# An encoder block on one Trainium2 core: two steps of the MLP's first product in plain float32 instead of split operands

## The chip, the cores and the metric

The kernel runs on one core of a Trainium2 chip, as one launch. A core has a matrix engine (TensorE, PE in the profile, with its weight loads PEld), a vector engine (DVE), a scalar engine (ACT), a general engine (GpSimd, POOL) and a queue engine (SyncE, SP), each with a program of its own that it runs in order, and 16 DMA engines between the main memory and the on-chip memory SBUF. Matrix products land in the banks of PSUM. The metric is the device time of one execution in microseconds (us), the median of several runs.

## The reference

One layer of a bidirectional encoder, 2048 rows of 1024 columns in float32. A mixing part (mLSTM heads and a long convolution) gives `mix`; then

```python
        mix = jnp.concatenate([y_m, y_h], axis=-1).astype(x.dtype) @ w_out
        x = x + rms_norm(mix, norm_mix_post)

        hm = rms_norm(x, norm_mlp_pre)
        ff = jnp.square(jax.nn.relu(hm @ w_mlp_in)) @ w_mlp_out
        x = x + rms_norm(ff, norm_mlp_post)
```

`w_mlp_in` is 1024 x 4096. The change is in the product `hm @ w_mlp_in`, the MLP's first.

## The kernel before

**Split products.** A float32 product is made of three matmuls of a faster type, fp32r. `split` writes each operand as hi + lo: hi is a cast (ACT, L166), lo the source less hi (DVE or POOL, L169). `mm3` then issues hi of one with lo of the other (L159), lo with hi (L160), hi with hi (L161). Given an operand that is not split, `mm3` issues one plain float32 matmul instead (L157); the profile shows a plain matmul as two records.

**Seven block products.** The first product is made in 32 steps. Step s takes the 256 columns number s % 16 of `w_mlp_in` and one half of the rows: the first half (1024 rows) in steps 0 to 15, the second in 16 to 31. A step is a 2 x 2 product by the Strassen-Winograd scheme: seven block products in the order 1, 2, 6, 5, 7, 4, 3, each of four blocks of 128 x 128 (weights) by 128 x 512 (rows). So a split step is 7 x 4 x 3 = 84 matmuls.

- The right operand of product i is one of seven combinations of the finished rows. `turn_out` (L1366 on) makes them for each pair of row blocks: PE turns the rows (L1373), DVE scales them (L1374), POOL combines them (L1389 to L1392), and they are stored to main memory in `ht`. `right_load` fetches combination i of a half into the tile that is to hold lo (named hm11 for i = 1, and so on), and `right_split` then puts hi into its other tile (hm10) and subtracts in place. Each split is made in two parts; the second goes to POOL where that is given. The seven operands of a half serve 16 steps.
- The weights of a step are made in `up_weights`: two loads (512 KB each), combinations on POOL (L1492, L1493, L1499, L1502), splits (ACT, POOL) into tiles of a pool named cb, which has nine places. A step's weights are split while the step before runs; its loads are issued a step earlier, after product 2 (`then`, in `up`).
- After each product DVE or ACT takes the result from its bank (L1669 for product 1 on ACT, L1656 for the others on DVE), the last sums are made at L1693 to L1695 and stored.

**The join with the output projection.** `out_proj` walks over 16 blocks of 128 rows. In each, POOL and DVE finish a group of `y` (L1267), PE turns it (L1273) and multiplies it with `w_out` (`part`: matmuls po), DVE and ACT evict with the norm (L1215 to L1221, in `post`), POOL adds the residual (L1222), ACT and DVE make the next norm (L1360 to L1363, in `normed`), and two rounds later the rows are turned out. PE, DVE and ACT follow the order in which this is written; POOL and SP follow the scheduler's. Step 0 of the first product is woven into the last rounds: `first_operands` loads hm1 and hm2, splits them, and loads, combines and splits the weights of step 0 after row blocks 11 to 14, in the scratch tiles wr and ws; `first_step` runs step 0 with tiles named m0 between the turns of row blocks 14 and 15, splitting hm6, hm5, hm7, hm4 and hm3 as they come. Steps from 1 on are `up`. At step 15, `then` loads the operands of the second half product by product, and splits them two products behind.

Of the kernel before, what the change touches and what calls it, by code (L numbers as in the profile page):

```python
# [8 lines left out]
F32 = mybir.dt.float32  # L9
F32R = mybir.dt.float32r  # L10
AF = mybir.ActivationFunctionType
ALU = mybir.AluOpType
# [135 lines left out]
class Builder:  # L148
# [1137 lines left out]
    def out_proj(self, c):  # L1286
# [129 lines left out]
        ys = {}  # L1416
        self.load(wb, io["norm_mix_post"].partition_broadcast(128))
        xns = {}
        staged = self.first_operands(scratch)
        wl = c.enter_context(tc.tile_pool(name="owl", bufs=2, side="right"))  # L1420
        for i in range(18):
            with tc.manual_schedule(engines={mybir.EngineType.PE,mybir.EngineType.DVE,mybir.EngineType.Activation}):
                if i == 0:
                    ys[1] = mixed(1)
                    zs[2] = gate(2)
                    part(pos[0], 0, ym[0], 0)
                    ym[1] = turned(ys.pop(1), 1, 1)
# [12 lines left out]
                if 0 < i < 16:  # L1440
                    xns[i - 1] = normed(i - 1, *done)
                    part(pos[i], 0, ym[i], 0)
                    if i + 2 < 16:
                        ys[i + 2] = mixed(i + 2)
                    if i > 1:
                        part(pos[i], 1, yz[i], 4)
                if 2 <= i:
                    turn_out(i - 2, xns.pop(i - 2))
                if i < 15:
                    part(pos[i], 1, ym[i], 0)  # L1450
                    done = finish(i, pos.pop(i))
                elif i == 15:

                    step = self.first_step(c, pp)
                    next(step)
                    part(pos[i], 1, ym[i], 0)
                    next(step)
                    rows = finish(i, pos.pop(i))
                    next(step)
                    xns[i] = normed(i, *rows)  # L1460
                else:
                    next(step)
            if 10 < i < 15:
                next(staged)
            if i == 14:
                gc.close()
            yield
        c.close()

# [13 lines left out]
    def up_weights(self, s, raw, s12, pieces=False):  # L1483
# [7 lines left out]
        cbs, cs = [], []  # L1491
        pool.tensor_tensor(s12[:, 0], a21, a22, ALU.add)  # L1492
        pool.tensor_tensor(a21, a11, a21, ALU.subtract)  # L1493
# [34 lines left out]
    def first_operands(self, scratch):  # L1528
# [9 lines left out]
        next(g)  # L1538
        yield
        self.w1_first = next(g)  # L1540
        yield

    def first_step(self, c, pp):

        wk = c.enter_context(self.tc.tile_pool(name="m0", bufs=1))
        count = [0]

        def tile(shape, tag):
            return wk.tile(list(shape), F32, tag=tag, name="m0", bufs={"g": 3, "s": 1, "r": 3}[tag])

        def bank():
            count[0] += 1
            if count[0] in (1, 2, 4, 5):
                return self.h1p.tile([128, 512], F32, tag="h1", name="pm")
            return pp.tile([128, 512], F32, tag="po", name="pm", bufs=3)

        for i in (6, 5):
            self.right_load(0, i)
        nxt = self.up_weights(1, [tile((128, 4, 256), "r") for _ in range(2)], tile((128, 2, 4, 128), "r"), True)
        next(nxt)  # L1560
        yield
        for i in (7, 4, 3):
            self.right_load(0, i)
        products = self.up_step(0, self.w1_first, lambda: tile((128, 2, 512), "g"), lambda: tile((128, 512), "s"), bank,
                                lambda i: None)
        next(products)
        next(products)
        self.right_split(6, self.pool)
        yield
        self.right_split(5, self.pool)  # L1570
        next(products)
        next(nxt)
        yield
        self.right_split(7)
        next(products)
        self.right_split(4)
        next(products)
        next(nxt)
        self.right_split(3)
        next(products)  # L1580
        yield
        for _ in products:
            pass
        self.w1 = next(nxt)
        yield

    def mlp(self):
        tc, io = self.tc, self.io
# [26 lines left out]
    def up(self, ring, next_bank, down):  # L1615
# [2 lines left out]

        def weights(s):
            raw = [ring((128, 4, 256), 1) for _ in range(2)]  # L1620
            g = self.up_weights(s % 16, raw, ring((128, 2, 4, 128), 1))
            next(g)
            return g

        def then(i):
            nonlocal nxt, w1
            if i == 2:
                if s + 1 < n:
                    w1 = next(nxt)
                if s + 2 < n:  # L1630
                    nxt = weights(s + 2)
            if s == 15:
                self.right_load(1, i)
                loaded.append(i)
            if len(loaded) > (2 if s == 15 else 0):
                j = loaded.pop(0)
                self.right_split(j, pool if j in (2, 7, 3) else None)
            if s == n - 1 and i in (2, 7):
                next(down)

        loaded = []
        w1, nxt = self.w1, weights(2)
        for s in range(1, n):
            for _ in self.up_step(s, w1, lambda: ring((128, 2, 512), 0),
                                  lambda: self.mk.tile([128, 512], F32, tag="mc", name="m4"), next_bank, then):
                pass

    def up_step(self, s, w, pair, single, next_bank, then):

        pe, dve, act, pool = self.pe, self.dve, self.act, self.pool  # L1650
        ga = self.ga[s % 16, s // 16]
# [11 lines left out]
        for i in (1, 2, 6, 5, 7, 4, 3):  # L1663
            pt = next_bank()
            hi, lo = self.hm[i]
            for k in range(4):
                self.mm3(pt, w(i, k), (hi[:, k, :], lo[:, k, :]), k == 0, k == 3)
            if i == 1:
                act.copy(c11, pt)  # L1669
            elif i == 2:  # L1670
# [248 lines left out]
```

## Time and profile before

| | us |
|---|---|
| median of 3 runs (2743.41 to 2745.59) | 2744.96 |
| the profiled run | 2740.85 |
| its span, from the first to the last instruction | 2738.9 |
| DVE busy in the span | 1529.3 |
| ACT busy | 1239.9 |
| POOL busy | 1218.2 |

The mean clock granted to PE is 0.981 of full speed. Rows of the timeline begin with the start and the length of a group of instructions; in square brackets stands how long the engine was idle before it, and what ended that. Matmuls overlap in the profile: the start of the next one says how long one takes. Rows of groups give the line, engine, operation, output and inputs with shapes, the count, the busy time, the mean in ns, and the idle time ahead of them.

### The profile page before, as it was taken

What the parts mean: (1) busy time and instruction counts of PE and PEld (TensorE: products, weight loads), DVE (VectorE), ACT (ScalarE), POOL (GpSimd) and SP (SyncE); (2) the same over time, 40 slices, a digit from 0 to 9 for tenths busy, and PEclk for the clock granted to TensorE, in tenths of its full rate; (3) what the DMA queues carried; (4) which work ended last, traced back from release to release, by engine and by line L of the source; (5) the groups of instructions that cost most, each with busy time, mean ns of one, the idle gap of its engine ahead of it and who ended that gap; (6) DMA issues with size and microseconds to landing.
All of it is one profiled execution on the core that took longest, in us unless ns stands there. A gap on an engine that the chain in (4) does not pass through costs nothing.

```text
span 2738.9 us, 35521 instructions
## 1 busy us (share of the span) xinstructions
PE 2604.2 (95%) x12293; PEld 2125.6 (78%) x12293; DVE 1529.3 (56%) x2453; ACT 1239.9 (45%) x2301; POOL 1218.2 (44%) x973
## 2 busy tenths in 40 slices
PE   6999999999899998889997999989999999999998
PEld 5778888777788887767775788868888888888876
DVE  5676653777446654765555444464445443543578
ACT  6355544555434445653433544354454233232244
POOL 1221124554225542456675877777773340311232
PEclk9999999999999999999998999989999999999999
DMA  6233346565665648546756444453446553445546
GB/s 173 59 97 107 113 122 226 183 191 175 203 216 180 191 156 273 166 145 209 239 165 220 149 168 143 167 210 139 162 144 253 176 182 110 123 143 164 181 160 222
DMA packets 288355, 465.76 MB, mean 170 GB/s; under 512 B 37542, under 2 KB 149414, under 8 KB 287152
## 3 DMA queue, kind: packets, MB, share of 16 engines
q1 hardware_dynamic: 227600, 324.85, 37.9%
q10 hardware_dynamic: 53264, 117.53, 11.4%
q0 software_dynamic: 7312, 21.11, 3.0%
q8 instruction: 98, 1.61, 0.2%
q14 instruction: 81, 0.66, 0.1%
HBM read 289.27 MB, written 174.13 MB: 169 GB/s over the span
## 4 chain that ended last, share of the span: by engine, by line
PE 40%; DVE 5%; POOL 3%; ACT 2%; DMA 2%; issue 2%; ACTq 0%; DVEq 0%; POOLq 0%; SPq 0%
PE pm L160 13%; PE pm L161 13%; PE pm L159 13%; DVE cb L169 1%; DVE hm L169 1%; POOL xt L1222 1%; ACT xo L1360 1%; DMA m<-in_w_mlp_out_dram 0%; DVE hm L1844 0%; POOL cb L169 0%; DVE xo L1363 0%; DMA hm<-ht 0%; ACTq L234 0%; DVE gss L1264 0%; POOL ht L1395 0%
## 5 line engine op out<-in xcount | busy, mean ns | idle before, releaser
L166 ACT CAST cb<-m 128x1024 fp32r<-128x1024 f32 (+1 forms) x346 | 281.3, 847 | 443.7 <-PE pm L159 388.6
L169 DVE TENSOR_TENSOR cb<-m,cb 128x1024 fp32r<-128x1024 f32 (+1 forms) x222 | 239.5, 1116 | 301.1 <-ACT cb L166 300.8
L160 PE MATMUL pm<-hm,cb 128*128 128x512 f32 x896 | 355.2, 396 | 18.8 <-DVE hm L169 14.7
L159 PE MATMUL pm<-hm,cb 128*128 128x512 f32 x896 | 354.5, 396 | 9.2 <-POOL cb L169 4.1
L161 PE MATMUL pm<-hm,cb 128*128 128x512 f32 x896 | 353.8, 395 | 0.0
L160 PE MATMUL pm<-cb 128*128 128x512 f32 x880 | 344.0, 391 | 6.5 <-DVE cb L169 6.5
L159 PE MATMUL pm<-cb 128*128 128x512 f32 x880 | 342.6, 390 | 1.0 <-DVE cb L169 1.0
L161 PE MATMUL pm<-cb 128*128 128x512 f32 x880 | 343.1, 390 | 0.0
L169 POOL TENSOR_TENSOR cb<-m,cb 128x1024 fp32r<-128x1024 f32 x124 | 268.7, 2180 | 71.0 <-ACT cb L166 71.0
L1656 DVE TENSOR_TENSOR m<-pm,m 128x512 f32<-128x512 f32 x224 | 154.4, 690 | 258.0 <-PE pm L161 231.3
L159 PE MATMUL pt<-hn,w 128*128 128x512 f32 x640 | 269.4, 421 | 1.0 <-ACT hn L486 0.9
L160 PE MATMUL pt<-hn,w 128*128 128x512 f32 x640 | 253.9, 397 | 0.7 <-DVE hn L487 0.7
L161 PE MATMUL pt<-hn,w 128*128 128x512 f32 x640 | 252.8, 395 | 0.0
L169 POOL TENSOR_TENSOR raw<-raw,hi 128x512 fp32r<-128x512 f32 x160 | 205.6, 1298 | 104.4 <-ACT hi L166 79.3
L160 PEld LDWEIGHTS pm<-hm,cb 128*128 128x128 f32 x896 | 170.6, 190 | 60.0 <-DVE hm L169 18.0
L159 PEld LDWEIGHTS pm<-hm,cb 128*128 128x128 f32 x896 | 170.7, 191 | 49.8 <-POOL cb L169 6.1
L160 PEld LDWEIGHTS pm<-cb 128*128 128x128 f32 x880 | 165.5, 188 | 44.0 <-DVE cb L169 9.8
L161 PEld LDWEIGHTS pm<-hm,cb 128*128 128x128 f32 x896 | 170.7, 191 | 36.3
L159 PEld LDWEIGHTS pm<-cb 128*128 128x128 f32 x880 | 165.4, 188 | 35.9 <-ACT junk L1829 1.4
L161 PEld LDWEIGHTS pm<-cb 128*128 128x128 f32 x880 | 165.6, 188 | 34.3
L1660 ACT ACTIVATE m<-m 128x512 f32<-128x512 f32 x128 | 80.5, 630 | 221.4 <-DVE m L1656 214.9
L159 PE MATMUL pt<-w,hn 128*128 128x260 f32 x512 | 156.8, 306 | 9.6 <-ACT w L166 9.6
(322 smaller groups left out, 5572.5 us busy)
## 6 DMA issues: line engine op xcount, KB each, us to landing
ga<-m ACTq DMA_DIRECT2D x96, 512.0 KB
m<-ga SPq DMA_DIRECT2D x96, 512.0 KB
d<-st ACTq DMA_DIRECT2D x64, 512.0 KB
m<-in_w_mlp_in_dram SPq DMA_DIRECT2D x62, 512.0 KB
m<-in_w_mlp_out_dram SPq DMA_DIRECT2D x114, 256.0 KB
raw<-d SPq DMA_DIRECT2D x96, 256.0 KB
xt<-in_x_dram SPq DMA_DIRECT2D x32, 512.0 KB
dk<-kst SPq DMA_DIRECT2D x32, 512.0 KB
```

Of the source, the lines that this page charges most:

```text
L159: pe.matmul(ps, w[1], x[0], start=first, stop=False)
L160: pe.matmul(ps, w[0], x[1], start=False, stop=False)
L161: pe.matmul(ps, w[0], x[0], start=False, stop=last)
L166: self.act.copy(hi, src)
L169: (eng_lo or self.dve).tensor_tensor(lo, src, hi.bitcast(F32), ALU.subtract)
L1222: eng.tensor_tensor(res[:, cs], tmp[e], res[:, cs], ALU.add)
L1360: act.activation(x1, xt, AF.Square, accum_out=ss1[:, h:h + 1])
L1656: dve.tensor_tensor(dst, a, b, ALU.add)
L1660: act.activation(g, g, AF.Relu)
```

## The change

Steps 0 and 16, the first of each half of the rows, use plain float32 matmuls (L157) of operands that are not split: the right operand as it was loaded, and the raw weights and their combinations.

- `up_weights` has a way `plain`: combinations L1492, L1493 and L1496 on POOL, and L1499 for product 3 once product 2 has read its operand; no split and no cb tiles.
- `first_operands` only loads w(0), after row block 14, into tiles m0. hm1 and hm2 are loaded after blocks 11 and 12. Nothing is split in `out_proj` before step 0.
- In steps 0 and 16 the right operands are split one product after they were read (`split_held`), those of products 2, 7 and 3 partly on POOL as before. The raw weights of step 1 lie in cb places, named m1.
- In step 16 the loads for step 18 are issued after product 3 instead of 2; in step 15 the second half's operands are loaded as before, and not split.

The evictions move from L1656 to L1667, the copy of product 1 from L1669 to L1681, the last sums from L1693 to L1705, L1502 to L1509.

```diff
@@ out_proj
-        staged = self.first_operands(scratch)
@@
-                    step = self.first_step(c, pp)
+                    step = self.first_step(pp)
@@
-            if 10 < i < 15:
-                next(staged)
+            if i in (11, 12):
+                self.right_load(0, i - 10)
             if i == 14:
                 gc.close()
+                self.first_operands(c)
@@ up_weights
+        if plain:
+            pool.tensor_tensor(s12[:, 1], s12[:, 0], a11, ALU.subtract)
+            places = {1: a11, 7: a21, 2: a12, 4: a22, 5: s12[:, 0], 6: s12[:, 1], 3: a12}
+            yield lambda i, k: places[i][:, k, :]
+            pool.tensor_tensor(a12, a12, s12[:, 1], ALU.subtract)
+            yield
@@ first_operands
-        for i in (1, 2):
-            self.right_load(0, i)
-        yield
-        self.right_split(1, self.pool)
-        yield
-        self.right_split(2, self.pool)
-        raw = [scratch("wr").rearrange("p (k f) -> p k f", k=4) for _ in range(2)]
-        g = self.up_weights(0, raw, scratch("ws").rearrange("p (i k f) -> p i k f", i=2, k=4))
+        raw = [m0.tile([128, 4, 256], F32, tag="r", name="m0", bufs=3) for _ in range(2)]
+        self.w_first = self.up_weights(0, raw, m0.tile([128, 2, 4, 128], F32, tag="r", name="m0", bufs=3), plain=True)
+        next(self.w_first)
@@ first_step
+        def then(i):
+            self.split_held()
+            self.held.append(i)
+            if i == 2:
+                next(self.w_first)
...
+        products = self.up_step(0, w, lambda: tile((128, 2, 512), "g"), lambda: tile((128, 512), "s"), bank, then, True)
@@ after first_step
+    def split_held(self):
+        if self.held:
+            j = self.held.pop(0)
+            self.right_split(j, self.pool if j in (2, 7, 3) else None)
@@ then, in up
-            if i == 2:
-                if s + 1 < n:
-                    w1 = next(nxt)
-                if s + 2 < n:
-                    nxt = weights(s + 2)
+            self.split_held()
+            if s == 16:
+                self.held.append(i)
             if s == 15:
                 self.right_load(1, i)
-                loaded.append(i)
-            if len(loaded) > (2 if s == 15 else 0):
-                j = loaded.pop(0)
-                self.right_split(j, pool if j in (2, 7, 3) else None)
+            if i == 2:
+                if s == 16:
+                    next(own)
+                if s + 1 < n:
+                    w1, own = next(nxt), nxt
+
+            if i == (3 if s == 16 else 2) and s + 2 < n:
+                nxt = weights(s + 2)
@@ up_step
-                self.mm3(pt, w(i, k), (hi[:, k, :], lo[:, k, :]), k == 0, k == 3)
+                x = lo[:, k, :].bitcast(F32) if plain else (hi[:, k, :], lo[:, k, :])
+                self.mm3(pt, w(i, k), x, k == 0, k == 3)
```

The order on the engines shows at three places. First POOL at the end of the output projection, before; L1222 is the residual, wr and ws are the raw weights of step 0 and their combinations:

```order
L1222 TENSOR_TENSOR xt_13926<-xo_13928,xt_13926 128x512
L169 TENSOR_TENSOR cb_14058<-wr_13947,cb_14057 128x1024
L1222 TENSOR_TENSOR xt_13926<-xo_13928,xt_13926 128x512
L169 TENSOR_TENSOR cb_14062<-wr_13948,cb_14061 128x1024
L1502 TENSOR_TENSOR wr_13948<-wr_13948,ws_13949 128x4x128
L169 TENSOR_TENSOR cb_14067<-ws_13949,cb_14066 128x1024
L169 TENSOR_TENSOR cb_14071<-wr_13948,cb_14071 128x512
L1222 TENSOR_TENSOR xt_14038<-xo_14040,xt_14038 128x512 x2
```

The same place on POOL after the change, with the raw weights in m0:

```order
L1222 TENSOR_TENSOR xt_13922<-xo_13924,xt_13922 128x512 x2
L1492 TENSOR_TENSOR m0_14048<-m0_14046,m0_14047 128x512
L1493 TENSOR_TENSOR m0_14046<-m0_14046 128x4x128
L1496 TENSOR_TENSOR m0_14048<-m0_14048,m0_14046 128x512
L1222 TENSOR_TENSOR xt_14025<-xo_14027,xt_14025 128x512 x2
```

The four splits between the residuals of two row blocks are gone, and the three combinations, which stood some rounds earlier, stand there instead.

Second, DVE in step 0 after the change, from the turn of row block 15 (L1363, L1374) to the first of the last sums; m0 are the results, pm the banks:

```order
L1363 TENSOR_SCALAR xo_14179<-xt_14177,r1_11971 128x1024
L1667 TENSOR_TENSOR m0_14160<-pm_14248,m0_14160 128x512
L1374 TENSOR_TENSOR xo_14179<-pto_14286,nw1_3584 128x512
L1667 TENSOR_TENSOR m0_14160<-pm_14234,m0_14160 128x512
L1374 TENSOR_TENSOR xo_14179<-pto_14292,nw1_3584 128x512
L169 TENSOR_TENSOR hm31_14156<-hm31_14156,hm30_14155 128x1024
L169 TENSOR_TENSOR hm51_14124<-hm51_14124,hm50_14123 128x1024 x2
L1667 TENSOR_TENSOR m0_14160<-pm_14261,m0_14160 128x512
L1667 TENSOR_TENSOR m0_14159<-pm_14309,m0_14159 128x512
L169 TENSOR_TENSOR hm71_14148<-hm71_14148,hm70_14147 128x1024
```

The split of hm3, whose product is the last of the step, stands ahead of those of hm5 and hm7 and ahead of the last two evictions (pm_14261 and pm_14309, products 4 and 3).

Third, PE at step 16 after the change, from the last matmul of step 15:

```order
L161 MATMUL pm_16483<-hm30_14155,cb_16259 128x512
L157 MATMUL pm_16514<-hm11_16374,m_16262 128x512 x4
L157 MATMUL pm_16520<-hm21_16391,m_16263 128x512 x4
L157 MATMUL pm_16549<-hm61_16420,m_16264 128x512 x4
L157 MATMUL pm_16562<-hm51_16438,m_16264 128x512 x4
L157 MATMUL pm_16572<-hm71_16459,m_16262 128x512 x4
L157 MATMUL pm_16585<-hm41_16480,m_16263 128x512 x4
L157 MATMUL pm_16598<-hm31_16509,m_16263 128x512 x4
```

28 plain matmuls on the raw tiles (hm11 and so on, m) stand where 84 on split ones stood.

More of the change, by code (lines that the diff above doesn't have):

```diff
@@ L1481, in hm_tile, with up_weights @@
         return self.hm_pool[i].tile(list(shape), dtype, tag=f"hm{i}{e}", name=f"hm{i}{e}")
[L1483 removed]
+    def up_weights(self, s, raw, s12, pieces=False, plain=False):
         act, pool = self.act, self.pool
@@ L1555, in bank, with place @@
             return pp.tile([128, 512], F32, tag="po", name="pm", bufs=3)
+        def place(shape):
+            return self.cb.tile(shape, F32, tag="cb", name="m1", bufs=9)
+        def then(i):
[3 more added lines that the diff above has]
+                next(self.w_first)
         for i in (6, 5):
             self.right_load(0, i)
-        nxt = self.up_weights(1, [tile((128, 4, 256), "r") for _ in range(2)], tile((128, 2, 4, 128), "r"), True)
+        w = next(self.w_first)
+        nxt = self.up_weights(1, [place([128, 4, 256]) for _ in range(2)], place([128, 2, 4, 128]), True)
         next(nxt)
@@ L1573, in first_step @@
         yield
-        self.right_split(7)
-        next(products)
-        self.right_split(4)
         next(products)
         next(nxt)
-        self.right_split(3)
         next(products)
+        next(products)
+        self.w1 = next(nxt)
         yield
@@ L1620, in weights @@
             raw = [ring((128, 4, 256), 1) for _ in range(2)]
-            g = self.up_weights(s % 16, raw, ring((128, 2, 4, 128), 1))
+            g = self.up_weights(s % 16, raw, ring((128, 2, 4, 128), 1), plain=s == 16)
             next(g)
```

26 lines of the change are left out of this document (9 added, 17 removed).

## Prediction

> **What bounds the kernel now.** I read the page's first part, then the windows by stage, then the waits and the timeline of TensorE around the two steps that change.
>
> ```profile
> PE 2604.2 (95%) x12293; PEld 2125.6 (78%) x12293; DVE 1529.3 (56%) x2453; ACT 1239.9 (45%) x2301; POOL 1218.2 (44%) x973
> ...
> 1449.00:1494.00 45.00, 29.41 (x105) 20.91 (x103) 30.38 (x27) 18.36 (x28) 26.88 (x20) 0.85 0.54 197
> 1600.00:1700.00 100.00, 100.00 (x441) 82.45 (x440) 45.48 (x58) 46.73 (x68) 75.23 (x43) 1.00 0.43 150
> 1784.00:1841.00 57.00, 47.02 (x171) 35.15 (x169) 39.54 (x37) 34.38 (x47) 45.61 (x22) 0.85 0.52 193
> ```
>
> TensorE (PE) is busy for 95% of the span, so as a whole it is the bound. In the windows (busy time of PE, PEld, DVE, ACT and POOL, then the granted clock) it is full and at clock 1.00 in the middle of the first product, 1600 to 1700, but idle for 15.6 of 45 us in step 0 and for 10 of 57 us in steps 16 and 17, with a clock of 0.85. Only such holes can be won.
>
> ```profile
> PE pm L160 <- DVE hm L169: 10.1, 4, 3.8
> PE pm L159 <- ACT hm L166: 4.1, 2, 3.3
> ...
> PE pm L160 <- DVE hm L169: 4.6, 3, 3.2
> PE pm L160 <- POOL hm L169: 3.5, 2, 2.2
> PE pm L159 <- POOL cb L169: 1.8, 2, 1.0
> ```
>
> The waits of PE (us in total, times, longest), two rows from 1449 to 1500 and three from 1784 to 1841, say on what: the splits of the right operands hm, which the change takes out of the way. How long the stages are, the timeline gives:
>
> ```profile
> 1449.83 0.39 PE L159 MATMUL pm<-hm,cb 128*128 128x512 f32 x1
> 1494.03 0.47 PE L159 MATMUL pm<-hm,cb 128*128 128x512 f32 x1 [0.88 <-POOL xo L1392]
> 1576.53 0.59 ACT L1669 COPY m<-pm 128x512 f32<-128x512 f32 x1 [0.71 <-PE pm L161]
> 1748.67 0.59 ACT L1669 COPY m<-pm 128x512 f32<-128x512 f32 x1 [0.71 <-PE pm L161]
> 1767.80 0.59 ACT L1669 COPY m<-pm 128x512 f32<-128x512 f32 x1 [0.71 <-PE pm L161]
> 1843.70 0.59 ACT L1669 COPY m<-pm 128x512 f32<-128x512 f32 x1 [0.18 <-PE pm L161]
> ```
>
> The first two rows are the first matmuls of steps 0 and 1: step 0 takes 44.2 us. The others are copies of a step's first product (the first matmul is 2.73 us earlier, a seventh of a step): of steps 5, 14, 15 and 18. A steady step is 1767.80 - 1748.67 = **19.13 us**. Steps 1 to 4 take 1573.80 - 1494.03 = 79.8 us, 3.3 over four steady ones. Step 15 ends at 1767.80 - 2.73 + 19.13 = 1784.2, step 18 begins at 1840.97: steps 16 and 17 take 56.8 us, **18.5 over** two steady ones.
>
> **The change, part by part.**
>
> *The plain products.* None is in this stage before; the nearest is an earlier line with the same shape:
>
> ```profile
> 1313.00 1.88 PE L1257 MATMUL py<-rd,s1i 128*128 128x512 f32 x4
> 1314.71 0.60 PE L1273 MATMUL ptp<-eye,ymt 128*128 128x128 f32 x4
> ```
>
> Four records of two plain matmuls take 1.71 us until the next operation: 0.855 us a matmul (two records each), against 19.13 / 84 = 0.228 for one of the 84 in a split step. A plain step is 28 x 0.855 = 23.94 us, **4.8 more** than a split one, 9.6 for two. That is sure; the gains below are net of it.
>
> *What a wait costs beside itself.*
>
> ```profile
> 1441.74 0.79 PE L159 MATMUL po<-wo,yt 128*128 128x512 f32 x1 [2.14 <-DVE xo L1221]
> 1442.33 0.63 PE L160 MATMUL po<-wo,yt 128*128 128x512 f32 x1
> 1442.75 0.63 PE L161 MATMUL po<-wo,yt 128*128 128x512 f32 x1
> ...
> 1445.25 0.40 PE L161 MATMUL po<-wo,yt 128*128 128x512 f32 x1
> 1445.48 0.39 PE L159 MATMUL po<-wo,yt 128*128 128x512 f32 x1
> ```
>
> After a pause of 2.14 us matmuls start 0.42 apart, and 0.23 again some 3.5 us later: about 1.5 us are lost behind each pause of over 2 us.
>
> *End of the output projection (gain 7, bounds 0 to 8).* Before, the operands of step 0 are prepared among its rows:
>
> ```profile
> 1401.70 1.60 POOL L1492 TENSOR_TENSOR ws<-wr 128x512 f32<-128x512 f32 x1
> 1403.38 1.29 POOL L1493 TENSOR_TENSOR wr<-wr 128x512 f32<-128x512 f32 x1
> 1404.63 1.75 POOL L1499 TENSOR_TENSOR ws<-ws,wr 128x512 f32<-128x512 f32 x1
> 1409.65 0.55 PE L1273 MATMUL ptp<-eye,ymt 128*128 128x128 f32 x3 [2.06 <-POOL ymt L1267]
> ...
> 1428.62 2.74 POOL L169 TENSOR_TENSOR cb<-wr,cb 128x1024 fp32r<-128x1024 f32 x1
> ```
>
> The three combinations keep POOL for 4.7 us just ahead of the L1267 that PE waits 2.06 for. The L169 of 2.74 us stands between the two halves of an L1222, and the chain from it (residual, norm, eviction L1221) ends in the wait of 2.14. Both blocks leave: (2.06 + 1.5) + (2.14 + 1.5) = 7.2. The new combinations stand after row block 14, ahead of one pair of L1222 only. I take 7.2; nothing if another engine is just as late. The moved load of w(0), two of 512 KB, now stands on SP between the x rows of blocks 14 and 15, in the one stretch where the DMA engines are full:
>
> ```profile
> 1440.00:1460.00 20.00, 15.11 (x60) 12.14 (x61) 9.64 (x10) 5.46 (x12) 14.77 (x15) 0.88 1.01 360
> ```
>
> At 360 GB/s it holds up what follows by 2.9 us at most, x of block 15 and hm6 first; both have more than that, as hm6 is split from 1454 on now and is wanted two products, 6.8 us, after step 0 begins. I cost it at nothing; without that cover it is the 2.9.
>
> *Step 0 to step 5 (gain 4, bounds +14 to -4).* Floor of step 0: 23.94 plus two turns of finished rows,
>
> ```profile
> 1446.17 1.04 PE L1373 MATMUL pto<-eye,xo 128*128 128x128 f32 x8
> ```
>
> 0.8 each, together 25.5, where 44.2 stood. What keeps it from the floor: (a) PE's seventh product reuses the bank of the second, so waits for DVE's eviction, some 1.8 us; (b) the last turn waits for L1363 of row block 15, behind the splits of hm1, hm2 and hm6 that ACT and DVE now do in these microseconds; (c) in the order of ACT, DVE and POOL the split of hm3 is placed ahead of those of hm5 and hm7, and can only begin when the last plain product has read hm3. DVE then does it, two splits of hm5 and an addition before the last eviction of step 0, for which step 1 waits:
>
> ```profile
> 1454.31 4.44 DVE L169 TENSOR_TENSOR hm<-hm,hm 128x1024 fp32r<-128x1024 f32 x1 [5.91 <-ACT hm L166]
> 1471.99 1.22 DVE L169 TENSOR_TENSOR hm<-hm,hm 128x1024 fp32r<-128x1024 f32 x1 [1.63 <-ACT hm L166]
> ```
>
> Three splits are 3.7 us at the short duration, 13 at the long one; I take the short. With 1.8 + 2 + 3.7 and 1.5 or so behind two of the pauses, step 1 begins some 36 us after step 0: 8 gained. Against that, w(2)'s second half is loaded only when DVE is done with an operand of step 0, and POOL, in its own order, does w(3)'s combinations ahead of w(2)'s last split:
>
> ```profile
> 1511.78 4.75 POOL L169 TENSOR_TENSOR cb<-m,cb 128x1024 fp32r<-128x1024 f32 x2
> ```
>
> Two such splits are 4.75 us, so steps 1 to 4 lose about 7.5 instead of 3.3: -4. Sum **4**. The bounds: nothing stalls (44.2 + 3.3 - 25.5 - 8), or step 1 begins no earlier than now.
>
> *Steps 16 and 17 (gain 12, bounds 7 to 13.7).*
>
> ```profile
> 1774.83 14.71 SPq L231 DMA_DIRECT2D hm<-ht  x14
> 1781.58 1.05 ACT L166 CAST hm<-hm 128x1024 fp32r<-128x1024 f32 x1 [13.19 <-DMA hm<-ht]
> ```
>
> The fourteen loads are issued from 1774.8 to 1789.5, the first is there at 1781.6, before step 16 begins at 1784.2; a plain product takes 3.42 us, the loads come about 2 us a product, so none is waited for. In PE's order nothing else stands in the way, so the floor is 23.94 + 19.13 = 43.1, 13.7 under 56.8. I leave 2 for the splits, which now share steps 16 and 17 with those of w(17) and w(18):
>
> ```profile
> L169 POOL TENSOR_TENSOR cb<-m,cb 128x1024 fp32r<-128x1024 f32 (+1 forms) x10 | 25.0, 2516 | 14.0 <-ACT cb L166 14.0
> L169 DVE TENSOR_TENSOR hm<-hm,hm 128x1024 fp32r<-128x1024 f32 x10 | 18.9, 1908 | 1.1 <-ACT hm L166 1.1
> L169 POOL TENSOR_TENSOR hm<-hm,hm 128x1024 fp32r<-128x1024 f32 x3 | 7.7, 2569 | 2.6 <-ACT hm L166 2.6
> ```
>
> *Sum:* 7.2 + 4 + 12 = 23.2 off the profiled run's 2740.85, or 2717.7. The median of the runs is 2744.96, 4.1 above the profiled one; the forecast is made against it: **2722**.
>
> **Rivals.**
>
> *Everything is hidden:* 8 + 14 + 13.7 = 35.7, **2709**. The full windows of steady steps speak for it, the reordering in (c) against it.
>
> *The queues give the first half back:* hm3's split ahead in three queues keeps step 1, and POOL's late w(2) and w(3) cost step 2 and 3. Steps 0 to 5 then lose 4, steps 16 and 17 gain only 9 as w(18) comes late in the same way: 7.2 - 4 + 9 = 12.2, **2733**. For it speaks 75.23 in 100 us of POOL already in steady steps.
>
> *DVE and POOL exclude each other.* DVE's split takes 4.44 us in one place and 1.22 in another, in the rows above, as if it stood still. POOL's steady work is 0.752 x 19.13 = 14.4 us a step; for steps 16 and 17 that is 28.8, plus POOL's three groups of hm 7.7 and DVE's eleven splits at 1.22, 13.4: 49.9 one after the other, more than 43.1. Then the second half gains 6.9 instead of 12, sum 18.1, **2727**. The Trainium skill, "SBUF — State Buffer", "Who interferes with whom", has this rule: a DVE instruction with two SBUF inputs contends with a GpSimd instruction that reads SBUF. The 4.44 agrees with it, but does not show whether all such pairs exclude each other.
>
> *Slower: the plain products run at the slow rate.* 0.42 against 0.23 a matmul would make a plain product of 4 x 0.855 cost 2.8 more; with all fourteen 39.8, so 2744.96 - 23.2 + 39.8 = **2762**. It decides from 9 products on, where the 23.2 are eaten. For it: both stages have a clock of 0.85 now. Against: L1257 ran at the quick rate, and a plain step has fewer reasons to pause. The Trainium skill, "TensorE: Matmul & The Clock Gate", "What's actually happening", has half clock only after an idle window of about 3.4 us; by that a pause of 2.14 us would cost nothing and the 7.2 above would be 4.2; here 2.14 us sufficed, so the trace decides.
>
> *It does not do what it says:* the raw operands come as late as the split ones, since w(0) and w(1) are loaded beside hm6 to hm3. Then step 0 is no shorter and pays 4.8; with 0 at the projection's end, -6 there and +7 in the second half, **2744**.
>
> **How the numbers follow.** The forecast 43%, all hidden 15, queues 18, exclusion 12, no effect 7, slow rate 5. The range 2709 to 2738 takes in all hidden, exclusion and queues, and the forecast with all three terms at their weak bounds but the first half at nothing (0 + 0 + 7 = 7). Over 0.2% (5.5 us, about what a measurement of this kernel can tell from no change) faster is 43 + 15 + 18 + 12 = 88, within 7, slower 5.
>
> **What would show it.** Right: step 0 of 34 to 38 us, its products 3.42 us apart, no wait of PE at L1267 and L1221 at the projection's end, steps 16 and 17 together 43 to 46. Wrong in (c): step 1's first matmul waits for DVE under 1 us or over 7. Queues: PE waits for cb splits at steps 2, 3 and 18. Exclusion: POOL and DVE never busy at once there, with DVE splits above 2 us. Slow rate: plain products over 6 us apart. No effect: plain products that wait for hm's DMA.

## The result, and the profile after

| | before, us | after, us |
|---|---|---|
| median (6 runs each) | 2745.47 (2743.41 to 2747.03) | 2731.7 (2727.73 to 2735.88) |
| the profiled run | 2740.85 | 2735.88 |
| its span | 2738.9 | 2733.9 |

The ratio is 0.995, with a 95% interval of 0.9939 to 0.996: 13.7 us faster (11 to 17). The two profiled runs stand only 5.0 apart. That is luck in a part which the change leaves alone, as the first matmul of the output projection's rows shows, in the timeline of PE before, and then after:

```profile
1196.81 1.22 PE L159 MATMUL po<-wo,y 128*128 128x512 f32 x2 [2.92 <-DVE y L169]
```

```profile
1202.06 0.73 PE L159 MATMUL po<-wo,y 128*128 128x512 f32 x2 [2.92 <-DVE y L169]
```

Every engine's instructions up to there are the same in both; in the 14 profiles of this study this start lies between 1196.8 and 1205.7, and the profiled run of before has the earliest. So from here on stages are compared by their own lengths. A stage's start is the first matmul of its first step; in the timeline of PE after, the starts of steps 0, 1, 5, 16 and 19 are these:

```profile
1447.63 2.74 PE L157 MATMUL pm<-hm,m 128*128 128x512 f32 x6
1487.96 0.77 PE L159 MATMUL pm<-hm,cb 128*128 128x512 f32 x1 [5.36 <-DVE m L1667]
1580.36 0.39 PE L159 MATMUL pm<-hm,cb 128*128 128x512 f32 x1
1790.75 0.59 PE L157 MATMUL pm<-hm,m 128*128 128x512 f32 x1
1854.98 0.39 PE L159 MATMUL pm<-hm,cb 128*128 128x512 f32 x1
```

Read in the same way in all kernels (P is the time from the rows' first matmul to step 0; the next columns are steps 0, 0 to 4, and 16 to 18; the first four rows are before, changed, and one half of the change each; each ratio is to the kernel of before as measured beside that run, with medians between 2745.28 and 2747.92):

```
                      P      0      0-4    16-18   median    ratio to before (95%)
before              253.0   44.2   123.8   75.9   2745.47
changed             245.6   40.3   132.7   64.2   2731.70   0.9950 (0.9939-0.9960)
second_half_only    255.0   43.8   123.4   64.9   2736.81   0.9962 (0.9949-0.9976)
first_half_only     244.5   39.5   131.8   75.9   2745.81   0.9991 (0.9981-1.0000)
changed_again       244.5   39.6   129.5   64.4   2734.09   0.9952 (0.9939-0.9964)
hm3_split_last      244.2   36.3   127.9   64.2   2730.31   0.9940 (0.9929-0.9952)
two_behind          244.6   31.1   124.8   64.5   2727.78   0.9936 (0.9924-0.9949)
splits_on_dve       244.0   34.1   121.8   64.5   2724.98   0.9927 (0.9915-0.9939)
w2_loaded_early     244.0   34.1   123.0   64.4   2727.82   0.9937 (0.9924-0.9950)
rows_before_w1      243.0   38.9   119.4   63.9   2720.20   0.9908 (0.9895-0.9922)
step1_in_order      243.8   37.2   119.4   63.9   2722.71   0.9919 (0.9904-0.9934)
step16_splits_on_dve 244.5  37.2   119.4   62.3   2719.74   0.9906 (0.9890-0.9923)
norm_first_in_order 244.1   36.7   117.0   64.0   2718.22   0.9899 (0.9884-0.9914)
all_together        244.1   36.7   116.9   62.3   2714.59   0.9884 (0.9861-0.9906)
```

Steps 5 to 15 take 210.4 us and steps 19 to 31 248.4 in all 14 profiles, so what differs stands in these columns or ahead of the rows. Kernels that have the same first half agree within 0.4 us in steps 0 to 4, except that the changed one has 132.7, 131.8 and 129.5 in three profiles; a difference of 2 or 3 us between two single profiles is weak evidence there.

The change took 9.0 from the projection's end (254.0, the mean of the two kernels with the old one, to 245.0, that of the two profiles of the changed kernel), gave back 7.5 in steps 0 to 4 (123.6 to 131.1), and took 11.6 from steps 16 to 18 (75.9 to 64.3). The sum, -13.1, is close to the 13.7 of the runs. The windows by stage after, steps 0, 1 to 4, and 16 to 18:

```profile
1447.00:1488.00 41.00, 28.69 (x77) 13.87 (x75) 27.93 (x27) 17.84 (x27) 25.11 (x16) 0.90 0.60 221
1488.00:1580.00 92.00, 83.71 (x335) 67.50 (x336) 47.75 (x46) 41.95 (x60) 76.98 (x46) 0.91 0.44 149
1790.00:1855.00 65.00, 63.69 (x229) 42.61 (x229) 47.12 (x44) 36.03 (x50) 50.81 (x25) 1.00 0.57 200
```

PE is now full, at clock 1.00, in the second half's start; in the first half's it still has holes of 12 and 8 us. The waits of PE after, 1440 to 1560 and then 1760 to 1850:

```profile
PE pm L159 <- POOL cb L169: 8.3, 2, 4.3
PE pto L1373 <- DVE xo L1363: 6.9, 1, 6.9
PE pm L159 <- DVE m L1667: 5.4, 1, 5.4
...
PE pm L159 <- POOL cb L169: 1.3, 2, 0.7
```

No wait is for a split of hm any more. In their place stand three others: the last row block's norm (L1363), the evictions of step 0 (L1667), and POOL's splits of w(2). What stood ahead of them shows POOL's own timeline after:

```profile
1473.40 2.12 POOL L1509 TENSOR_TENSOR m<-m,m 128x512 f32<-128x512 f32 x1
1482.73 2.80 POOL L169 TENSOR_TENSOR hm<-hm,hm 128x1024 fp32r<-128x1024 f32 x1 [7.21 <-ACT hm L166]
1491.02 2.48 POOL L169 TENSOR_TENSOR hm<-hm,hm 128x1024 fp32r<-128x1024 f32 x1 [5.49 <-ACT hm L166]
...
1496.39 1.62 POOL L1389 TENSOR_TENSOR tb<-xo 128x512 f32<-128x512 f32 x1
...
1507.41 1.70 POOL L1492 TENSOR_TENSOR m<-m 128x512 f32<-128x512 f32 x1
...
1512.14 4.68 POOL L169 TENSOR_TENSOR cb<-m,cb 128x1024 fp32r<-128x1024 f32 x2 [0.44 <-ACT cb L166]
...
1518.14 1.30 POOL L1492 TENSOR_TENSOR m<-m 128x512 f32<-128x512 f32 x1
...
1522.88 6.80 POOL L169 TENSOR_TENSOR cb<-m,cb 128x1024 fp32r<-128x1024 f32 x3
```

POOL stood idle for 7.2 and 5.5 us ahead of the splits of hm3 and hm7, whose casts came late, with the combination of the last rows (L1389) behind them, which had its input from about 1479 on, when DVE's L1374 was done. It came to w(2) (L1492) at 1507.4, 59.8 us after the start of step 0, and not for a late load, as no idle time stands ahead of that row. Before the change POOL stood idle in step 0 as well, 6.6 and 8.8 us for casts of w(1), and came to w(2) after 58.1. So the idle time is not new: step 0 became 4 us shorter, and w(2) came no earlier.

PE's two waits for POOL have different causes. The first, 4.3 us at the start of step 2 (1514.5), is for the first of the two splits at 1512.14. The second, 4.0 us inside step 2 (1525.7), is for the split at 1522.88, ahead of which POOL made the combinations of w(3) (L1492 at 1518.14, then L1493 and L1506), 4.7 us.

The waits are only half of the loss. Behind each of these pauses matmuls start 0.43 us apart instead of 0.23 for some time, as here behind the 5.4 us at the start of step 1, where it lasts 5.7 us:

```profile
1488.52 0.63 PE L160 MATMUL pm<-hm,cb 128*128 128x512 f32 x1
1488.95 0.63 PE L161 MATMUL pm<-hm,cb 128*128 128x512 f32 x1
```

In steps 1 to 4 this holds for 35 matmuls and costs 7.1 us, beside 8.3 us of waits (28 matmuls, 5.7 us and 7.0 us in the second profile).

### The profile page after: what moved, and what is told of

The parts are those of the page before. It is cut to its first block, busy times and chain, and to the rows that moved or that the text cites. A ratio compares the mean times of both kernels' runs of the same rounds, so it can differ in the third digit from the quotient of the medians.

```text
span 2733.9 us, 35402 instructions
## 1 busy us (share of the span) xinstructions
PE 2608.9 (95%) x12237; PEld 2116.4 (77%) x12237; DVE 1551.1 (57%) x2454; ACT 1231.8 (45%) x2293; POOL 1204.4 (44%) x964
## 4 chain that ended last, share of the span: by engine, by line
PE 40%; DVE 5%; POOL 3%; DMA 2%; issue 2%; ACT 1%; ACTq 0%; DVEq 0%; POOLq 0%; SPq 0%
PE pm L159 13%; PE pm L160 13%; PE pm L161 13%; DVE cb L169 1%; POOL cb L169 1%; PE po L159 1%; DVE hm L169 1%; DMA m<-ga 1%; PE po L161 1%; PE po L160 1%; DMA m<-in_w_mlp_in_dram 1%; POOL xt L1222 0%; DVE hm L1856 0%; DVE hm L1786 0%; DMA out_dram<-hm 0%
## 5 line engine op out<-in xcount | busy, mean ns | idle before, releaser
L169 DVE TENSOR_TENSOR cb<-m,cb 128x1024 fp32r<-128x1024 f32 (+1 forms) x222 | 237.4, 1106 | 299.8 <-ACT cb L166 299.5
L159 PE MATMUL pm<-hm,cb 128*128 128x512 f32 x840 | 331.6, 395 | 15.0 <-POOL cb L169 9.6
L160 PE MATMUL pm<-hm,cb 128*128 128x512 f32 x840 | 330.1, 393 | 0.0
L161 PE MATMUL pm<-hm,cb 128*128 128x512 f32 x840 | 329.9, 393 | 0.0
L169 POOL TENSOR_TENSOR cb<-m,cb 128x1024 fp32r<-128x1024 f32 x120 | 265.2, 2221 | 55.5 <-ACT cb L166 55.5
L1667 DVE TENSOR_TENSOR m<-pm,m 128x512 f32<-128x512 f32 x224 | 153.7, 690 | 223.3 <-PE pm L161 212.2
L160 PE MATMUL pt<-hn,w 128*128 128x512 f32 x640 | 254.0, 397 | 0.7 <-DVE hn L487 0.7
L169 POOL TENSOR_TENSOR raw<-raw,hi 128x512 fp32r<-128x512 f32 x160 | 205.8, 1298 | 103.7 <-ACT hi L166 78.5
L159 PEld LDWEIGHTS pm<-hm,cb 128*128 128x128 f32 x840 | 159.4, 190 | 51.6 <-POOL cb L169 11.3
L160 PEld LDWEIGHTS pm<-hm,cb 128*128 128x128 f32 x840 | 159.5, 190 | 34.7 <-DVE hm L169 0.3
L161 PEld LDWEIGHTS pm<-hm,cb 128*128 128x128 f32 x840 | 159.1, 189 | 34.2
```

The lines of the kernel that those rows point to most:

```text
L159: pe.matmul(ps, w[1], x[0], start=first, stop=False)
L160: pe.matmul(ps, w[0], x[1], start=False, stop=False)
L161: pe.matmul(ps, w[0], x[0], start=False, stop=last)
L169: (eng_lo or self.dve).tensor_tensor(lo, src, hi.bitcast(F32), ALU.subtract)
L1667: dve.tensor_tensor(dst, a, b, ALU.add)
```

## The experiments

**The two halves apart, and the change again.** `second_half_only` has the projection and step 0 of before, and step 16 plain; `first_half_only` the reverse; `changed_again` is the changed kernel. The core of the first two edits, against the changed kernel:

```diff
@@ second_half_only (out_proj, first_operands and first_step are those of before)
-        m0 = self.m0 = c.enter_context(self.tc.tile_pool(name="m0", bufs=1))
+        for i in (1, 2):
+            self.right_load(0, i)
...
@@ first_half_only (weights, then and the loop of up)
-            g = self.up_weights(s % 16, raw, ring((128, 2, 4, 128), 1), plain=s == 16)
+            g = self.up_weights(s % 16, raw, ring((128, 2, 4, 128), 1))
...
+            if len(loaded) > (2 if s == 15 else 0):
+                j = loaded.pop(0)
+                self.right_split(j, pool if j in (2, 7, 3) else None)
```

> The changed kernel once more, for a second profile and more times. In the two profiles steps 0 to 4 went from 123.8 to 132.7 us, steps 16 to 18 from 75.9 to 64.2, and the end of the output projection gained 2.2: together 5.0, while the medians differ by 13.8. Theory A (the profile's loss in the first half is real, and the profiled run of the changed kernel, the slowest of its six, lost some 4 us more than usual in one place): 2728 to 2736 us, and in this profile steps 0 to 4 take 127 to 129 us. Theory B (the stages are the same in each run, and the 9 us are spread over the whole span): steps 0 to 4 take 132 to 133 us again, steps 16 to 18 take 64.

> Only step 16 is plain; the output projection and step 0 are as before. Theory A and B alike: steps 16 to 18 take 64 us where 75.9 stood, so 11.7 less than before, 2734 us. If the first half of the change loses 6.7 us as the two profiles say, this kernel is faster than the changed one by about that; if the first half gains the 2 us that the medians leave for it, it is 2 us slower than the changed one.

> Only step 0 is plain, with the projection's end as changed; step 16 is as before. By the two profiles: 2.2 gained, 8.9 lost, so 6.7 us slower than before, 2752 us. By the medians, 2 us faster than before, 2743.

Measured: 2734.09, 2736.81 and 2745.81, against 2747.92 for before on that chip. The stages repeat: steps 0 to 4 took 129.5 and 131.8, steps 16 to 18 took 64.4 and 64.9. The loss in the first half is real, as both theories had it; in size the 129.5 stand between theory A (127 to 129) and B (132 to 133), nearer to A, and the 131.8 of `first_half_only` near B. What neither had is where the missing time is: the projection's rows take 244.5 in both kernels that have the new ones and 255.0 in the one with the old, which the later start of the rows in the first profile had hidden. The second half carries the change: 10.4 us by the ratio (6.6 to 14), with 11.0 in steps 16 to 18. The first half as a whole is worth 2.5 us (0 to 5.2), the 2 that the medians had left for it, though its interval reaches down to nothing; by the stages it is 9.0 - 7.5 = 1.5.

**The split of hm3 at the end of step 0.**

```diff
         for _ in products:
             pass
+        self.split_held()
         yield
```

> The changed kernel with the split of hm3 written at the end of step 0, so that it stands behind those of hm5, hm7 and hm4 on ACT, DVE and POOL. Theory (the order is the cause: DVE has three splits ahead of step 0's last evictions, and POOL stands idle 7.2 and 5.5 us behind hm3's and hm7's casts before it can finish w(1) and turn to w(2)): the wait of 5.4 us at step 1 goes to under 1, the 8.3 us of waits for POOL at step 2 to under 4, and steps 0 to 4 take some 122 us instead of 132.7. Rival 1 (DVE and POOL exclude each other): splits of 3 us stay, under 4 us gained. Rival 2 (the load of w(2), which waits for DVE's last sum of step 0): the 5.4 goes, but the 8.3 at step 2 stays, and 5 are gained.

Measured: 36.3 instead of 40 for step 0, but 127.9 instead of 131 for steps 0 to 4, where 122 was expected. The waits of PE, 1440 to 1560:

```profile
PE pto L1373 <- DVE xo L1363: 6.2, 1, 6.2
PE pm L160 <- DVE hm L169: 5.4, 2, 4.8
PE pm L159 <- POOL cb L169: 2.6, 1, 2.6
PE pm L159 <- DVE m L1668: 2.4, 1, 2.4
```

The wait at step 1 fell from 5.4 to 2.4, which the order of DVE explains. The waits for POOL fell from 8.3 to 2.6: only L1492 of w(3) now stands ahead of w(2)'s third split, and step 2 took 21.1 us instead of 27.6. But step 1 waited inside instead, 5.4 us for DVE's splits, and step 2 began only 68.2 us after step 0 (66.9 in the changed kernel). One of these splits took 6.6 us beside POOL's work, and those ahead of L1363 still took 3.0 and 3.3, as rival 1 had it; the gain of 3.2 on the mean of the changed kernel fits that rival, not the theory. POOL now stood idle 12.2 us for hm7's cast alone. So hm3 was one item of a queue that was long altogether.

**Two products behind; and no splits for POOL.** `two_behind` lets splits of step 0 run two products behind instead of one. `splits_on_dve` keeps one, and gives POOL none of them (`shared` is set where `up` begins):

```diff
@@ two_behind, then of first_step
-            self.split_held()
             self.held.append(i)
+            if len(self.held) > 2:
+                self.split_held()
...
+        while self.held:
+            self.split_held()
@@ splits_on_dve, split_held
-            self.right_split(j, self.pool if j in (2, 7, 3) else None)
+            self.right_split(j, self.pool if j in (2, 7, 3) and self.shared else None)
```

> As hm3_split_last, and in step 0 the splits run two products behind instead of one, so that the last row block's L1363 stands ahead of the split of hm6 on DVE and ACT. Step 0 took 36.3 us with a wait of 6.2 at the last turn. Theory (the splits ahead of L1363 hold up the turn): the wait falls to about 3 and step 0 to some 33 us; steps 0 to 4 gain less, since step 1's end waits for POOL's w(2) and that is no earlier: 125 to 128 us instead of 127.9, time within 3 of hm3_split_last. Rival (the chain from the residual to the norm itself is the bound): the wait stays at 6.

> As hm3_split_last, but in step 0 all splits of hm are DVE's; POOL gets none (7.7 us less work for POOL, 3 x 1.2 more for DVE if they run alone). Theory of the order (POOL stood idle 12.2 us for a split of hm7 whose cast came late, and only then turned to w(1), the last rows and w(2)): step 2 starts 5 to 8 us earlier after step 0's start than the 68.2 of hm3_split_last, steps 0 to 4 take about 121 us. Rival (exclusion of DVE and POOL is what binds): the sum of their work is what counts, the gain is about 3 x 1.3, so 124. Rival (the load of w(2), issued when DVE has done the last sum of step 0): no gain at step 2, 127.

Measured: `two_behind` 31.1 for step 0, with a wait for L1363 of 2.4, so the splits ahead of it were that wait; but step 1 then took 34.3 against 31.9, and steps 0 to 4 took 124.8. `splits_on_dve`: 121.8 for steps 0 to 4, 6.1 less than `hm3_split_last`. It has no wait for POOL's hm, of which `two_behind` had one of 2.5:

```profile
PE pm L159 <- POOL cb L169: 4.8, 2, 4.6
PE pto L1373 <- DVE xo L1363: 4.1, 1, 4.1
PE pm L160 <- DVE hm L169: 3.2, 3, 1.5
```

The forecast for the queue, 121, was met within 1; exclusion alone had 124, the load 127. Step 2 began 62.4 us after step 0 instead of 68.2. POOL's idle time, though, is still there: 11.5 us instead of 12.2, now for the cast of w(1)'s combinations. POOL came to w(2) 6.7 us sooner for the most part because it had 7.7 us of splits less to do.

**The load of w(2), and POOL's order.** `w2_loaded_early` lays out the tiles of step 0 so that the raw tiles of w(2) do not reuse its results. `rows_before_w1` adds the second edit:

```diff
@@ w2_loaded_early, first_operands
-        raw = [m0.tile([128, 4, 256], F32, tag="r", name="m0", bufs=3) for _ in range(2)]
+        raw = [m0.tile([128, 4, 256], F32, tag="q", name="m0", bufs=1)]
+        self.pair0 = [m0.tile([128, 2, 512], F32, tag="g", name="m0", bufs=3)]
+        raw.append(m0.tile([128, 4, 256], F32, tag="r", name="m0", bufs=2))
@@ rows_before_w1, first_step
         next(products)
-        self.w1 = next(nxt)
         yield
+        self.w1 = next(nxt)
         for _ in products:
```

> As splits_on_dve, with step 0's tiles laid out so that the raw tiles of w(2) lie where step 0's weights were, not its results: the second load of w(2) no longer waits for DVE's last sum. If the load is the bound of step 2: steps 0 to 4 take 5 us less than in splits_on_dve. If POOL's order is (it does w(1) and the last rows first): the same within 1 us, though the load lands some 20 us earlier.

> As w2_loaded_early, with the last splits of w(1) written after the turn of row block 15, so that POOL combines the last rows (L1389 to L1392) before it waits for the cast of w(1)'s combinations. If POOL's order is the bound, POOL begins w(2) about 5 us earlier and steps 0 to 4 take some 5 us less than in w2_loaded_early, 112 to 115 us; time about 2718. If the sum of POOL's work is the bound, 1 us or nothing.

Measured: the load is not the bound. Steps 0 to 4 took 123.0 instead of 121.8, where 5 less would have shown it, and POOL came to w(2) at the same point, 51.3 us after step 0's start, straight from the combination of the last rows. The medians of these two kernels differ by 2.8 the other way, and the one has runs from 2723.7 to 2733.1; no gain can be read. With the rows combined first, steps 0 to 4 took 119.4, 3.6 less where 5 was expected (and 112 to 115 in all), although step 0 became 4.8 longer. POOL came to w(2) 40.0 us after the start of step 0 instead of 51.3, but then stood idle 11.8 us for ACT's casts of it, so that its first split of w(2) began only 2.8 us sooner (57.5 instead of 60.3): the next bound is ACT's order. The waits of PE:

```profile
PE pm L159 <- POOL cb L169: 6.8, 2, 6.0
PE pto L1373 <- DVE xo L1363: 4.0, 1, 4.0
```

One wait of 6.0 us is new, at step 1's start. In the built order a single matmul of step 1's product 5 had moved ahead of the step's first product, and it needs the split of w(1)'s combinations.

**Step 1 in its written order.** PE's part of step 1 is fixed to the order of the code, nothing else:

```diff
-            for _ in self.up_step(s, w1, lambda: ring((128, 2, 512), 0),
+            with self.tc.manual_schedule(engines={mybir.EngineType.PE}) if s == 1 else nullcontext():
+                for _ in self.up_step(s, w1, lambda: ring((128, 2, 512), 0),
```

> As rows_before_w1, with PE's matmuls of step 1 kept in the order in which they are written: in rows_before_w1 one matmul of product 5 of step 1 had come to stand ahead of the step's first product, and PE waited 6.0 us for its weights. If that is the cause of the 6.0, step 1 starts 5 us sooner after step 0's start, and steps 0 to 4 take 114 to 115 us instead of 119.4. If POOL's work is the bound of step 2 all the same, the 5 come back there and the sum stays at 118 to 119.

Measured: 119.4 again, where 114 to 115 was expected of the misplaced matmul. Step 1 began 1.7 us sooner after step 0, not 5. The wait moved from POOL to DVE, as the waits show:

```profile
PE pm L159 <- DVE m L1675: 4.5, 1, 4.5
PE pto L1373 <- DVE xo L1363: 4.0, 1, 4.0
PE pm L159 <- POOL cb L169: 1.8, 1, 1.8
```

So the misplaced matmul was not the cause: DVE's evictions end no sooner (37.0 us after the start of step 0 in both), and the splits ahead of them are slow. DVE's timeline in `rows_before_w1`, where that is the same, and behind it POOL's:

```profile
1457.64 2.36 DVE L169 TENSOR_TENSOR hm<-hm,hm 128x1024 fp32r<-128x1024 f32 x2 [0.42 <-ACT hm L166]
...
1472.11 5.45 DVE L169 TENSOR_TENSOR hm<-hm,hm 128x1024 fp32r<-128x1024 f32 x2 [1.70 <-ACT hm L166]
1477.48 1.27 DVE L1674 TENSOR_TENSOR m<-pm,m 128x512 f32<-128x512 f32 x2
```

```profile
1471.54 1.35 POOL L1390 TENSOR_TENSOR tb<-xo,tb 128x512 f32<-128x512 f32 x1
1472.76 1.36 POOL L1392 TENSOR_TENSOR xo<-xo 128x512 f32<-128x512 f32 x1
1473.99 1.34 POOL L1391 TENSOR_TENSOR tb<-xo,tb 128x512 f32<-128x512 f32 x1
```

Two splits took 2.36 us mostly beside an idle POOL, and 5.45 beside POOL's L1390 to L1391. The combination that was moved forward for POOL's sake falls on DVE's splits of hm5, and those stand ahead of the evictions.

**The rest.** `step16_splits_on_dve` has no split of hm for POOL in step 16 either. `norm_first_in_order` is `step1_in_order` with step 0's splits two products behind. `all_together` is both.

```diff
@@ step16_splits_on_dve, up
-        self.shared = True
@@ norm_first_in_order, then of first_step
-            self.split_held()
             self.held.append(i)
+            if len(self.held) > 2:
+                self.split_held()
...
+        while self.held:
+            self.split_held()
```

> As step1_in_order, with the splits of step 16's operands on DVE alone too. Theory (POOL's queue makes step 18's weights late: waits for POOL's cb of 0.9 to 1.6 us and 1.5 to 2 us lost at step 18): steps 16 to 18 take 62 us (23.6 + 19.3 + 19.1) instead of 64.0. Rival (the weights come late because their loads were issued later, after product 3): 64 as before.

> As step1_in_order, with step 0's splits two products behind (as in two_behind). If the wait for L1363, 4.0 us, is lost time of its own: step 0 takes 3 us less and steps 0 to 4 about 2 less. If DVE's work up to step 1's products is the bound (two_behind paid 3.9 us of waits for splits in step 1): step 0 is shorter, step 1 longer by the same, and the sum stays within 1 us.

> norm_first_in_order and step16_splits_on_dve together. The two act in stages 300 us apart, so they should add: steps 0 to 4 in 117 us, steps 16 to 18 in 62.3, 1.7 us faster than norm_first_in_order. Rival (the start of the second half hangs on what is left over from the first): 64 at steps 16 to 18.

Measured: steps 16 to 18 took 62.3, with step 18 at 19.13 instead of 20.7: POOL's splits of hm had made w(18) late by these 1.6 us, not the later load. `norm_first_in_order`: step 0 took 36.7 instead of 37.2 and steps 0 to 4 117.0 instead of 119.4, about the 2 of the first theory, but not where it had them: the wait for L1363 is still 3.6, and most of the gain is in steps 1 and 2 (41.9 instead of 44.0). The two add, 116.9 and 62.3, and the kernel with both is the fastest: **2714.59 us, 0.9884 of before (0.9861 to 0.9906)**, some 18 us under the changed kernel. What is left in it, PE's waits from 1440 to 1560:

```profile
PE pm L159 <- DVE m L1676: 4.1, 1, 4.1
PE pto L1373 <- DVE xo L1363: 3.6, 1, 3.6
PE pm L160 <- DVE hm L169: 0.8, 1, 0.8
```

## Why the prediction was right, and where it was not

The direction and the range were right, the size was not: 13.7 measured, 23.2 forecast. The measured 2731.7 lies 10 from the forecast's 2722 and 1.3 from the 2733 of the rival of the queues; the range held because it took in that rival. Of the signs it named, products 3.43 us apart and 43.2 us for steps 16 and 17 came; step 0 in 34 to 38 us and an end of the wait at L1221 did not. By its terms:

- **The plain product: right.** 3.43 us each in steps 0 and 16 where nothing waits (eight records 0.429 apart), so 24.0 for step 16, where 23.94 was forecast. By the first matmul of step 17 step 16 takes 23.63 and step 17 19.56: that record begins 0.03 us after the last plain one, so 0.4 us stands in the wrong step.
- **The second half: right.** 12 forecast, 11.6 measured, with no wait in step 16, as the arithmetic of the loads had it. Steps 16 and 17 took 43.2 us, 0.1 over the floor. The 2 us left for shared splits came at step 18 instead, 1.9 to 2.0 in the changed kernel, and `step16_splits_on_dve` shows that POOL's part of the splits was the cause.
- **The projection's end: right in size, in part by the wrong rows.** 7.2 forecast, 9.0 measured. It was built on two waits, for L1267 and for L1221. The waits of PE from 1195 to 1447, before and then after:

```profile
PE py L1257 <- DVE xo L1374: 3.9, 2, 2.0
...
PE ptp L1273 <- POOL ymt L1267: 2.9, 2, 2.1
...
PE po L159 <- DVE xo L1221: 2.7, 2, 2.1
PE ptp L1273 <- DVE yt L169: 1.3, 1, 1.3
```

```profile
PE po L159 <- DVE xo L1221: 2.9, 2, 2.2
PE ptp L1273 <- POOL ymt L1267: 1.3, 2, 0.9
```

The wait of 2.1 for L1267 is gone, as forecast. That for L1221 is still there (2.2), at another row block. In its place went 3.9 for L1374 and 1.3 for L169, between 1355 and 1377 us, which the prediction leaves out; why they went is not shown. All waits in these two views fell from 18.2 to 12.9 us, and the stage by 7.4 in these two profiles; the rest, and the 9.0 of the means, is not itemised.

- **Steps 0 to 4: wrong, and this is the step that failed.** "Sum 4" was gained on paper; 7.5 were lost, 11.5 apart, while the two other terms were 1.4 off together. Two terms of it failed.

  *Step 0 was to take 36 and took 40, since its queue on DVE was priced at the short duration.* The bank of the second product (a) did not show among the waits. The turn behind L1363 (b) was put at 2 and PE waited 6.9: the two splits of hm6 and L1363 itself took 2.97, 3.29 and 1.75 us beside POOL's work, 4.8 more than the 1.22, 1.22 and 0.75 that they take alone. The three splits ahead of the evictions (c) were put at 3.7; they took 5.6, and PE waited 5.4. `two_behind`, with those of hm6 behind L1363, had 2.4 at that turn.

  *Steps 1 to 4 were to lose 7.5 and lost 92.4 - 76.5 = 15.9 (13.3 in the second profile).* The waits alone are 8.3 (7.0). The prediction charged 1.5 us of slow matmuls behind the pauses of step 0, and nothing for them in steps 1 to 4, where they cost 7.1 (5.7). Of its two causes for the waits the late load was not one (`w2_loaded_early`). The combinations of w(3) were, for 4.0 of the 8.3. For the other 4.3 it had not asked when POOL would come to w(2): no earlier than before, so that a shorter step 0 only brought PE to weights that were not there. It had followed (c) through DVE to PE, and not through POOL, which kept w(1), the last rows and w(2) behind splits of hm. `hm3_split_last`, `splits_on_dve` and `rows_before_w1` take 131 down to 119.4 by order and by who does the splits; how much of that is POOL's queue and how much DVE's stretched splits is not separated.

- **The rivals.** "The queues give the first half back" is what happened in the first half, and more so: it had 4 lost in steps 0 to 4, and 9 gained in the second half, where 11.6 were; that its time is met so closely is luck, as the two misses cancel. Exclusion of DVE and POOL was a true mechanism in the wrong place: in steps 16 and 17 nine of the eleven splits on DVE took 1.6 to 3.4 us, but PE waited for none, and in the first half it did. The slow rate for plain products was seen only behind the pause of 6.9 us, where the first two records of the last product start 0.86 and 0.85 us apart and the product takes 4.5 us; the others took 3.43, so it cost 1 us and not 39.8.
- **Its readings.** A step's first matmul is 2.93 us ahead of the copy of its first product, not 2.73, so steps 1 to 4 took 79.6 before, 3.1 over four steady ones, and fourteen times 2.8 is 39.2; neither changes a conclusion.

## What to carry to other kernels

When work is taken off an engine's critical place and put "behind" something, follow it through the queue of every engine that gets a part, and ask what stands idle behind it there: a split that waits for a late cast blocks all that is ready behind it. Price that queue by the durations that its parts have beside the engines then at work, and count what PE loses behind a pause as well as the pause. A change made in two places is worth measuring in each, as one half can carry it and the other give back. And compare stages by their own lengths: two profiled runs can differ by more in parts that did not change than the change is worth.

## What the runs showed of the hardware

DVE's subtractions of two SBUF tiles (the splits of hm) take 1.21 to 1.23 us when no tensor operation of POOL runs beside them, in all 99 such cases of the 14 profiles. In the other 234 the median is 2.1, with up to 4.44 in the kernel before and 8.8 in `two_behind`. In the changed kernel, from the timelines of DVE and then of POOL:

```profile
1464.26 1.22 DVE L169 TENSOR_TENSOR hm<-hm,hm 128x1024 fp32r<-128x1024 f32 x1 [1.12 <-ACT hm L166]
1468.14 2.97 DVE L169 TENSOR_TENSOR hm<-hm,hm 128x1024 fp32r<-128x1024 f32 x1 [2.66 <-DMA x<-xt]
...
1471.11 3.29 DVE L169 TENSOR_TENSOR hm<-hm,hm 128x1024 fp32r<-128x1024 f32 x1
1474.33 1.75 DVE L1363 TENSOR_SCALAR xo<-xt,r 128x1024 f32<-128x1024 f32 x1
...
1480.97 5.64 DVE L169 TENSOR_TENSOR hm<-hm,hm 128x1024 fp32r<-128x1024 f32 x3 [1.75 <-ACT hm L166]
```

```profile
1470.27 3.05 POOL L169 TENSOR_TENSOR cb<-m,cb 128x1024 fp32r<-128x1024 f32 x1 [0.24 <-ACT cb L166]
1473.40 2.12 POOL L1509 TENSOR_TENSOR m<-m,m 128x512 f32<-128x512 f32 x1
```

The split of 3.29 us begins in POOL's 3.05 and ends 1.0 us after POOL has begun the next; L1363, which takes 0.75 beside an idle POOL, took 1.75 here and 2.82 in `rows_before_w1`. Evictions with one input in PSUM do not slow: the page after has

```profile
L1667 DVE TENSOR_TENSOR m<-pm,m 128x512 f32<-128x512 f32 x224 | 153.7, 690 | 223.3 <-PE pm L161 212.2
```

a mean of 690 ns over all 224, none below 673 or above 694, with POOL busy for 474 of the 661 us from 1447 to 2108. This agrees with the Trainium skill, "SBUF — State Buffer", "Who interferes with whom", by which a DVE instruction with two SBUF inputs contends with a GpSimd instruction that reads SBUF, and one with at most one SBUF input, outside the 2-port modes, does not. L1363 has one tensor input and slowed; no run here shows in which mode it ran.
